# A small transfer ahead of the first load of a row-normalizing kernel

## The chip, the cores and the metric

The kernel runs on one core of one Trainium2 chip. The metric is the device time of one execution in microseconds (us). Before the change it is 81.85 us (median of 3 runs, 81.74 to 81.93). Every time of a whole kernel quoted below is a median of executions in the fast state; a span, a landing or a packet is read from a single profile. A ratio is the mean time of one kernel's fast runs over that of the other's of the same rounds, so it is not quite the ratio of the medians that stand beside it. The span of a profile is shorter than the device time (79.9 us against 81.77 us in the profiled run of before). A profile is a single execution; as the experiments will show, spans of such single executions differ by 0.1 to 0.2 us without any difference in the medians.

## The reference

```python
def setup_inputs():
    batch, dim = 1024, 4096
    return {"x": np.random.randn(batch, dim).astype(np.float32), "axis": -1, "eps": np.float32(1e-12)}

def reference(x, axis, eps):
    norm = np.sqrt(np.sum(x ** 2, axis=axis, keepdims=True) + eps)
    return (x / norm).astype(np.float32)
```

Each of 1024 rows of 4096 numbers is divided by its own length: 16.8 MB are read and 16.8 MB written.

## The kernel before

The rows are cut into two groups of 512, four rows on each of 128 partitions. Each group is one load of 8.4 MB and one store of 8.4 MB, both issued by SyncE. All of x fits into on-chip memory, so no buffer is ever waited for. In the profiles DVE is VectorE, ACT is ScalarE and POOL is GpSimd; a q behind an engine's name (SPq, ACTq, PEq) marks its instruction queue, from which transfers are issued. `to_front` moves both load instructions into the program's entry block, ahead of the barrier at which the engines meet, so that SyncE issues them as its first two instructions.

```python
eps_t = scratch_pool.tile([P, 1], F32)
nc.vector.memset(eps_t, eps)
sq_act = scratch_pool.tile([P, D], F32)
sq_dve = scratch_pool.tile([P, D], F32)
scratch = {"act": sq_act, "dve": sq_dve}

groups = []
for i in range(n_tiles):                       # n_tiles = 2
    g = RowGroups(nc, io, stats, scratch, D, R, eps_t)
    load = nc.sync.dma_start(out=g.flat(), in_=x_t[i])
    to_front(nc, load.ins)
    groups.append(g)

for i, g in enumerate(groups):
    # ... squares with row sums on ACT and DVE, square root, reciprocal, scaling ...
    store = nc.sync.dma_start(out=out_t[i], in_=g.flat())
```

## Time and profile before

| quantity, from the profile of before | value |
|---|---|
| span | 79.9 us |
| DVE busy, ACT busy | 26.7 us (33%), 29.7 us (37%) |
| data moved, mean rate | 33.55 MB, 420 GB/s |
| SyncE's issue of the first load | 0 to 0.38 us |
| first packets begin | from 1.0 us |
| landing of the first load (first squares start) | 21.81 us |
| landing of the second load | 41.14 us |
| first store issued, second store issued | 38.7 us, 56.5 us |

A transfer is carried by 16 DMA engines. Each takes 8 packets of 64 KB of it, then a completion write of 4 bytes. An issue is the SyncE instruction that starts a transfer; its record in the profile doesn't contain the movement of the data. The prediction below shows the lines that bear on this and how to read them. The head is its word for the part of the first load's time in which the DMA engines are not yet full. What it calls a ring is one DMA engine's part of an issuing engine's queue.

### The profile page before, as it was taken

The page shows a single profiled execution, that of the slowest core. Times are in us where ns is not written, and L with a number is a line of the kernel's source. Part 1 is how long each engine was busy: PE and PEld are TensorE (multiplying, and loading weights), DVE is VectorE, ACT ScalarE, POOL GpSimd, SP SyncE. Part 2 cuts the span into 40 slices and gives each one's busy share as a digit, 9 for nine tenths or more (in the row PEclk, how much of TensorE's full clock was granted, in tenths as well). Part 3 has the DMA queues.
Part 4 walks back from the last instruction along what each step waited for, and adds up shares of the span by engine and source line. Part 5 has one row for each costly group of instructions (what it writes and reads, how often), then busy time and mean ns, then how long its engine had stood idle before and what let it go on. Part 6 is the DMA issues. An engine that isn't in the chain of part 4 may idle for free.

```text
span 79.9 us, 93 instructions
## 1 busy us (share of the span) xinstructions
DVE 26.7 (33%) x21; ACT 29.7 (37%) x23; POOL 0.2 (0%) x4
## 2 busy tenths in 40 slices
DVE  0000000000099599960049995999200000000000
ACT  3200000000099999989349999950000000000000
POOL 1000000000000000000000000000000000000000
DMA  9099996599996699993899991999974999965990
GB/s 492 33 525 525 525 525 295 230 525 525 525 525 262 262 525 525 525 525 164 361 525 525 525 459 66 525 525 525 525 328 197 525 525 525 525 295 230 525 525 0
DMA packets 576, 33.55 MB, mean 420 GB/s; under 512 B 64, under 2 KB 64, under 8 KB 64
## 3 DMA queue, kind: packets, MB, share of 16 engines
q1 hardware_dynamic: 576, 33.55, 97.6%
HBM read 16.78 MB, written 16.78 MB: 420 GB/s over the span
## 4 chain that ended last, share of the span: by engine, by line
DMA 51%; ACT 10%; DVE 9%; SPq 0%; issue 0%
DMA xt<-in_x_dram 51%; ACT sq_act L33 9%; DVE xt L64 9%; ACT rstd L53 1%; SPq L219 0%; DVE rstd L59 0%
## 5 line engine op out<-in xcount | busy, mean ns | idle before, releaser
L33 ACT ACTIVATE sq_act<-xt 128x4096 f32<-128x4096 f32 x6 | 21.7, 3609 | 21.7 <-DMA xt<-in_x_dram 21.7
L42 DVE SCALAR_TENSOR_TENSOR sq_dve<-xt 128x4096 f32<-128x4096 f32 x2 | 8.8, 4424 | 25.7 <-DMA xt<-in_x_dram 25.7
L64 DVE TENSOR_SCALAR xt<-xt,rstd 128x4096 f32<-128x4096 f32 x7 | 16.5, 2353 | 0.2
L72 ACT ACTIVATE xt<-xt,rstd 128x3584 f32<-128x3584 f32 x1 | 3.3, 3282 | 0.2 <-DVE rstd L59 0.2
L53 ACT ACTIVATE rstd<-ssq,eps_t 128x1 f32<-128x1 f32 x8 | 2.1, 289 | 0.1
L59 DVE RECIPROCAL rstd<-rstd 128x1 f32<-128x1 f32 x8 | 1.3, 159 | 2.4 <-ACT rstd L53 2.4
L33 ACT ACT_TABLE_LOAD x1 | 1.3, 1283 | 1.3 <-PEq L257 1.3
L53 ACT ACT_TABLE_LOAD x1 | 1.3, 1283 | 0.0
L33 ACT ACTIVATION_READ_ACCUMULATOR sq_act<-xt 128x1 f32 x6 | 1.1, 186 | 0.0
L211 DVE MEMSET eps_t<- 128x1 f32 x1 | 0.1, 59 | 1.3 <-PEq L257 1.3
L78 DVE TENSOR_SCALAR xt<-xt,rstd 128x512 f32<-128x512 f32 x1 | 0.5, 486 | 0.0
L42 DVE DVE_READ_ACCUMULATOR sq_dve<-xt 128x1 f32 x2 | 0.2, 82 | 0.0
L257 POOL MEMSET const-bfloat16-1.0<- 128x1 bf16 x1 | 0.1, 103 | 0.0
L257 POOL MEMSET const-uint8-127<- 128x1 uint8 x1 | 0.1, 102 | 0.0
L257 POOL MEMSET const-float32-0.0<- 128x1 f32 x1 | 0.1, 100 | 0.2 <-issue 0.2
L257 POOL MEMSET const-float32-1.0<- 128x1 f32 x1 | 0.1, 99 | 0.0
## 6 DMA issues: line engine op xcount, KB each, us to landing
xt<-in_x_dram SPq DMA_DIRECT2D x2, 31.2
out_dram<-xt SPq DMA_DIRECT2D x2, 22.5
```

What stands on the lines that cost most here:

```text
L33: self.nc.scalar.activation(out=sq_a, in_=self.x[:, r], func=ACT_F.Square, accum_out=self.ssq[:, r : r + 1],)
L42: self.nc.vector.scalar_tensor_tensor(out=sq_v, in0=self.x[:, r], scalar=1.0, in1=self.x[:, r], op0=ALU.mult, op1=ALU.mult, accum_out=self ...
L53: self.nc.scalar.activation(out=self.rstd[:, r : r + n], in_=self.ssq[:, r : r + n], func=ACT_F.Sqrt, bias=self.eps_t,)
L59: self.nc.vector.reciprocal(out=self.rstd[:, r : r + n], in_=self.rstd[:, r : r + n])
L64: self.nc.vector.tensor_scalar_mul(out=self.x[:, r], in0=self.x[:, r], scalar1=self.rstd[:, r : r + 1])
L72: self.nc.scalar.activation(out=self.x[:, r, :cut], in_=self.x[:, r, :cut], func=ACT_F.Copy, scale=rstd,)
L78: self.nc.vector.tensor_scalar_mul(out=self.x[:, r, cut:], in0=self.x[:, r, cut:], scalar1=rstd)
L211: nc.vector.memset(eps_t, eps)
L257: nc = _bacc.Bacc("TRN2", target_bir_lowering=False, num_devices=1)
```

## The change

A tile of 16 partitions by 128 numbers (512 bytes each, 8 KB together) is loaded from the first rows of x by the same queue, ahead of both loads. Nothing reads the tile. The intent can only be to let the small transfer pay whatever a queue's first use costs, so that the large load finds the queue awake.

```diff
     scratch = {"act": sq_act, "dve": sq_dve}
+
+
+    first = scratch_pool.tile([16, D // 32], F32)
+    to_front(nc, nc.sync.dma_start(out=first, in_=x[:16, : D // 32]).ins)
 
     groups = []
```

## The prediction

> **What bounds the kernel now.** I read four things in this order: the page's table of DMA issues and its chain of work, then the DMA share by long stretches, then the same view in short stretches at the head of the span and at the three borders between transfers, then what the DMA issues and their landings look like.
>
> The chain of work that ended last, and two rows of the page:
>
> ```profile
> ## 4 chain that ended last, share of the span: by engine, by line
> DMA 51%; ACT 10%; DVE 9%; SPq 0%; issue 0%
> ...
> xt<-in_x_dram SPq DMA_DIRECT2D x2, 31.2
> out_dram<-xt SPq DMA_DIRECT2D x2, 22.5
> ```
>
> The chain runs load, load, squares and scalings of the second group, second store. It is misleading: it says that arithmetic (ACT 10%, DVE 9%) holds the end, because the last store's issue waits for the last scaling. But that store was issued at 56.5 us and took 23.3 us to land, for 8.4 MB. It stood behind the first store. So I looked at what the DMA engines do meanwhile. The columns of the next view are: stretch, its length, busy time of DVE, ACT and POOL with their number of instructions, granted clock, DMA share (1.00 is all 16 engines busy), GB/s.
>
> ```profile
> 0.00:4.00 4.00, 0.06 (x1) 1.28 (x1) 0.20 (x4) 1.00 0.74 262
> 4.00:20.90 16.90, 0.00 (x0) 0.00 (x0) 0.00 (x0) 1.00 1.00 434
> 20.90:40.20 19.30, 12.45 (x10) 16.55 (x12) 0.00 (x0) 1.00 1.00 435
> 40.20:59.60 19.40, 14.23 (x10) 11.87 (x10) 0.00 (x0) 1.00 1.00 432
> 59.60:78.90 19.30, 0.00 (x0) 0.00 (x0) 0.00 (x0) 1.00 1.00 435
> ```
>
> From 4 us to 78.9 us all 16 DMA engines are full, through both loads and both stores. The bound is the one DMA queue, at 435 GB/s. The page counts 576 packets for 33.55 MB, 64 of them under 512 B (the completion writes, 16 for each of four transfers); so 512 data packets of 65,536 B, 8 for each engine and transfer. Arithmetic is hidden. Only the head is not full, so the head is what the change can touch. In short stretches (this view books a packet, with its bytes and its whole duration, where it begins, so a share above 1 is normal):
>
> ```profile
> 0.00:1.00 1.00, 0.00 (x0) 0.00 (x0) 0.20 (x4) 1.00 0.00 0
> 1.00:1.30 0.30, 0.00 (x0) 0.04 (x1) 0.00 (x0) 1.00 7.24 2403
> 1.30:1.60 0.30, 0.06 (x1) 0.30 (x1) 0.00 (x0) 1.00 1.13 437
> 1.60:2.10 0.50, 0.00 (x0) 0.50 (x1) 0.00 (x0) 1.00 0.91 393
> ...
> 4.00:4.60 0.60, 0.00 (x0) 0.00 (x0) 0.00 (x0) 1.00 4.03 1748
> ```
>
> Bytes give the number of packets that begin: 2403 GB/s x 0.30 us / 65,536 B = 11, then 2, then 3: the 16 first packets. Share times length times 16 engines over that number gives their mean duration: 7.24 x 0.30 x 16 / 11 = 3.16 us for the 11 early ones, 2.71 us for the two, 2.43 us for the last three. In the stretch from 4.0 to 4.6 us 16 packets begin, of 4.03 x 0.60 x 16 / 16 = 2.42 us. So 2.42 us is the steady time, and the early first packets take 0.74 us longer. An engine that begins at 1.1 us and takes 3.16 us ends at 4.3 us; one that begins at 1.9 us and takes 2.43 us ends at 4.3 us too. Read as steady packets, data flows from about 1.9 us on every engine, however early its first packet began.
>
> **The head in numbers.** The first squares start on the first load's landing, at 21.81 us. Eight steady packets are 8 x 2.42 = 19.3 us. The head is the rest, 2.5 us: the issue, 0.38 us, then 0.6 us until packets begin (1.0 us), 0.9 us until data flows, and 0.4 us to 0.6 us for the spread of the engines and the completion. The issue's row:
>
> ```profile
> L219 SPq DMA_DIRECT2D xt<-in_x_dram x2: 383/404/426, 0.0 to 0.4; - x2
> ```
>
> **What the Trainium skill says.** "DMA: Bandwidth & Descriptors", Queues, rings and completion order: what one sequencer issues goes to one ring on each DMA engine, and descriptors are consumed in ring order. The trace agrees as far as it goes: at 20.9 to 21.5 us, with the first load's last packets ending, 16 packets of the second begin (4.04 x 0.60 x 16 / 16 = 2.42 us each), nothing between. So the small transfer really is ahead of the load on every ring it touches. The same page, on why a DMA increments its semaphore by 16: the slowest dimension decides how many engines take part, and 16 rows give all 16. So each engine would get one row of 512 B and a completion write. No run here shows this yet. "Perfetto Trace Analysis", DMA Instruction — HWDGE: the issue's record covers the wait for the descriptor generator and the making of descriptors, not the data. The trace agrees: the record ends at 0.38 us, the first packet begins after 1.0 us. The DMA page's Specifications give some 0.6 us to the first byte on this path; here it is 1.0 - 0.38 = 0.6 us.
>
> **The change, part by part.** Nothing is removed. The order of instructions shows the one addition, on SyncE, ahead of the two loads; no compute engine's order changes, and both loads and stores keep shape and place. Nobody on the way to the stores waits for the small tile.
>
> Added, the issue: the four issues here take 0.34 to 0.43 us although all carry the same 128 rows, so I have no row for 16. I take the same cost, some 0.38 us plus the 0.05 us that lies between the two loads' issues (0.00 to 0.86 us for 383 + 426 ns): 0.43 us. The loads' issues move back by that, on the path.
>
> Added, the data: 512 B on each engine, at 65,536 B in 2.42 us, is 0.02 us. The completion write costs little at a border: transfers follow each other at 19.33 us (landings 21.81 and 41.14) against 19.34 us for eight packets, so nothing of size hides there. Together under 0.05 us.
>
> Moved: the start barrier behind the issues comes 0.4 us later, so the table load on ACT starts at 1.7 us instead of 1.26 us. It is needed at 21.8 us; it costs nothing.
>
> Possible gain: the 0.9 us between the first packet's beginning and the flow. If this is a first-use cost of the rings or of memory, the small packets start at 1.0 us, pay it until 1.9 us, and the load, whose packets can begin at 1.4 us, flows from 1.9 us. Then the late issue is hidden: 0 to +0.1 us. If it is the ordinary latency of any read at an idle ring, the load pays it again from 1.4 us: +0.43 us. If the small transfer costs less to issue and takes the whole cost away, the load flows from 1.4 us: -0.5 us.
>
> Since the queue is full from there on, whatever the head gains or loses moves all four transfers by as much. The arithmetic moves with the first landing: the first store is issued at 38.7 us, with load packets running to 40.8 us, so there is about 1 us of reserve after its own issue and start latency, and it keeps that when both move together.
>
> **The rivals.** (a) *Plain addition*, +0.4 us, 82.3 us. For it: three of the first packets, begun last, took only 2.43 us, so there is no fixed price for a ring's first packet; early packets seem merely to wait for something that comes at the same distance from the issue, which would move with the issue. (b) *First-use cost absorbed*, about 81.9 us: the ends of all first packets lie within half a microsecond however they began, which suits one common event started by the first packet of all. (c) *Warm-up pays*, 81.3 to 81.5 us: this is what the change hopes for. Against it: SyncE issues one after the other, so the load can't begin before 1.4 us. (d) *The completion write of the small transfer holds the load's packets* until its data is confirmed, +0.5 to 1 us, 82.4 to 82.9 us: against it stand the borders, where packets of the next transfer follow without a gap. (e) *A bound elsewhere*: none is in sight, since compute is 33% and 37% of the span.
>
> **Range and chances.** I weigh (a) 0.45, (b) 0.3, (c) 0.15, (d) 0.1. The mean is +0.45 x 0.4 + 0 - 0.15 x 0.45 + 0.1 x 0.8, about +0.2 us: 82.0 us. Eight in ten: 81.4 to 82.6 us, with 0.1 us for the spread of the runs. Two per cent are 1.64 us. To win that, the head of 2.5 us would have to shrink to 0.9 us, less than issue plus first byte; to lose it, the small transfer would have to cost four issues. Within 2%: 0.97; faster 0.01; slower 0.02.
>
> **What would show each step.** In the changed profile: three issues on SyncE ahead of everything, each of about 0.4 us (a short first one proves my issue cost wrong); 16 more packets of 512 B and 16 completion writes, beginning at 1.0 us; the load's first packets beginning at 1.4 us or later. Their mean duration decides between the rivals: 3.0 us again for (a), near 2.4 us for (b) and (c); steady packets from about 2.3 us for (a), 1.9 us for (b), 1.4 us for (c). The first squares start at 22.2, 21.9 or 21.4 us, the second load lands 19.3 us later in each, and the end moves by the same. If the second landing or the stores move by something else, then the claim that the queue is one full pipe is wrong.

## The result, and the profile after

The changed kernel takes 82.36 us (82.21 to 82.69, 6 runs) against 81.86 us (81.74 to 81.93, 6 runs) in the same rounds. The ratio is 1.0066 with a 95% interval of 1.0047 to 1.0085. So it is slower by about half a microsecond: clear of the noise, but well within 2%. The span of the profiled run grew from 79.94 us to 80.38 us, by 0.44 us. (That run, at 82.21 us, was the fastest of the six.)

The start of the changed kernel's timeline (start, duration, both in us, then what ran):

```profile
0.00 0.39 SPq L218 DMA_DIRECT2D first<-in_x_dram  x1
...
0.44 0.89 SPq L223 DMA_DIRECT2D xt<-in_x_dram  x2
1.74 1.28 ACT L33 ACT_TABLE_LOAD   x1 [1.74 <-PEq L261]
...
22.24 3.62 ACT L33 ACTIVATE sq_act<-xt 128x4096 f32<-128x4096 f32 x1 [19.22 <-DMA xt<-in_x_dram]
```

The small issue takes 0.39 us of SyncE's time, as much as a load of 8.4 MB, and the first load's issue starts at 0.44 us instead of 0. The first load then lands at 22.24 us instead of 21.81 us: 0.43 us later. From its own issue to its landing it takes 21.80 us, as before. The table load on ACT, which waits for the start barrier, came 0.47 us later and cost nothing.

The DMA engines at the head of the changed kernel (columns as in the prediction: stretch, length, DVE, ACT, POOL, clock, DMA share, GB/s):

```profile
1.00:1.40 0.40, 0.00 (x0) 0.00 (x0) 0.00 (x0) 1.00 0.09 21
1.40:1.90 0.50, 0.06 (x1) 0.16 (x1) 0.00 (x0) 1.00 6.28 2097
1.90:4.00 2.10, 0.00 (x0) 1.12 (x1) 0.00 (x0) 1.00 0.00 0
4.00:4.50 0.50, 0.00 (x0) 0.00 (x0) 0.00 (x0) 1.00 0.00 0
4.50:5.00 0.50, 0.00 (x0) 0.00 (x0) 0.00 (x0) 1.00 4.84 2097
```

The small packets begin at 1.0 us, where the load's packets began before. They are tiny: a share of 0.09 over 0.40 us is 0.036 us for each engine, completion write included. The load's 16 first packets begin between 1.4 and 1.9 us (2097 GB/s x 0.50 us / 65,536 B = 16), and their mean duration is 6.28 x 0.50 x 16 / 16 = 3.14 us. So the waiting that made the first packets long before is there in full; before, the mean of all 16 was (11 x 3.16 + 2 x 2.71 + 3 x 2.43) / 16 = 2.97 us. The second packets begin between 4.5 and 5.0 us, against 4.0 to 4.6 us before.

From there on nothing differs. The long stretches, each set some 0.45 us later than those of before:

```profile
0.00:4.50 4.50, 0.06 (x1) 1.28 (x1) 0.20 (x4) 1.00 0.70 235
4.50:21.40 16.90, 0.00 (x0) 0.00 (x0) 0.00 (x0) 1.00 1.00 434
...
60.05:79.40 19.35, 0.00 (x0) 0.00 (x0) 0.00 (x0) 1.00 1.00 434
```

The page's count of packets went from 576 to 608: 16 of 512 B and 16 completion writes, so the small transfer did use all 16 engines.

```profile
DMA packets 608, 33.56 MB, mean 418 GB/s; under 512 B 80, under 2 KB 96, under 8 KB 96
```

### The profile page after: what moved, and what is told of

Read it like the earlier page. It is cut to its first block, busy times and chain, and to the rows that moved or that the text cites. A ratio compares the mean times of both kernels' runs of the same rounds, so it can differ in the third digit from the quotient of the medians.

```text
span 80.4 us, 95 instructions
## 1 busy us (share of the span) xinstructions
DVE 26.7 (33%) x21; ACT 29.7 (37%) x23; POOL 0.2 (0%) x4
## 4 chain that ended last, share of the span: by engine, by line
DMA 51%; ACT 10%; DVE 9%; SPq 1%; issue 0%
DMA xt<-in_x_dram 51%; ACT sq_act L33 9%; DVE xt L64 9%; ACT rstd L53 1%; SPq L223 1%; SPq L218 0%; DVE rstd L59 0%
```

## The experiments

My theory after this result: the change costs the time that SyncE takes to issue one more transfer ahead of the first load, and next to nothing else. It takes nothing away from the load's start. The rivals: the small packets or their completion writes hold what is behind them (D); or a gain from the warm-up exists, and the late issue ate it (W). Ten kernels were run. Those of one batch ran on one chip and share the runs of before: 81.81 us (9 runs) for the first three below and the one with the second load behind the barrier, 81.78 us (7 runs) for the pair behind the barrier, the changed addresses and the first load in halves, 81.89 us (7 runs) for the last two.

### The small transfer between the two loads

```diff
         groups.append(g)
+        if i == 0:
+            first = scratch_pool.tile([16, D // 32], F32)
+            to_front(nc, nc.sync.dma_start(out=first, in_=x[:16, : D // 32]).ins)
```

> The same small transfer, issued between the two loads instead of ahead of both. Theory (the cost is SyncE's issue time ahead of the first load): the first load is issued at 0 again and lands at 21.8 us as before; the second load's issue is hidden; the time is that of before, +0.02 to +0.1 us for 512 B and a completion write on each engine between the loads' packets. Rival (the small transfer's packets or its completion write hold the packets behind them): +0.4 to +0.5 us, now seen as a gap between the two loads' packets at 21 us.

Measured: 81.93 us, ratio 1.0017 (1.0004 to 1.0030). The added 0.12 us of the medians is a quarter of the change's cost. The transfer is the same and its packets run on the same engines; only the order of two issues differs. The first squares of this profile start at 21.93 us, 0.12 us later than in before's, though nothing extra is ahead of that load: this is the spread between single profiles. Between the last packet of the first load and the first of the second the trace shows some 0.03 us on each engine, where the small packet and the second completion write lie. So the data of a small transfer costs about 0.03 us here, and D falls as the explanation of 0.5 us for a queue that is already busy. For the start of an idle queue, the runs behind the barrier, below, decide.

### Two small transfers ahead

```diff
     to_front(nc, nc.sync.dma_start(out=first, in_=x[:16, : D // 32]).ins)
+    more = scratch_pool.tile([16, D // 32], F32)
+    to_front(nc, nc.sync.dma_start(out=more, in_=x[16:32, : D // 32]).ins)
```

> Two small transfers ahead of the first load. Theory: two issues of 0.39 us and their gaps, so 0.89 to 0.93 us more than before and the first load's packets from 1.9 us on, about 82.8 us. Rival (a once-only cost or a partly absorbed start): the second one costs clearly less or more than the first, which cost 0.44 us of the span.

Measured: 82.78 us against 81.81 us, ratio 1.0112 (1.0097 to 1.0128). The medians differ by 0.97 us, twice the change's 0.50 us.

```profile
0.00 0.39 SPq L218 DMA_DIRECT2D first<-in_x_dram  x1
...
0.44 0.41 SPq L220 DMA_DIRECT2D more<-in_x_dram  x1
0.90 0.90 SPq L225 DMA_DIRECT2D xt<-in_x_dram  x2
```

The first load is issued at 0.90 us. The cost grows with the issues ahead of it; the second small transfer costs what the first one did, so nothing of the first one's cost was made good by a once-only gain.

### The small transfer on ScalarE's queue

```diff
-    to_front(nc, nc.sync.dma_start(out=first, in_=x[:16, : D // 32]).ins)
+    to_front(nc, nc.scalar.dma_start(out=first, in_=x[:16, : D // 32]).ins)
```

(In this run `to_front` was changed too: it places an instruction in the entry block of the engine that issues it, where before it always took SyncE's place.)

> The same small transfer, issued at the front of ScalarE's queue, so that SyncE issues the first load at once. Theory: within 0.1 us of before, as SyncE's issue of 0.39 us is off the path. Rival 1 (data or completion on the engines costs): +0.4 us stays, as the small packets still run on all 16 engines around 1 us. Rival 2 (a warm-up gain exists, and was eaten by the issue): 0.2 to 0.7 us faster than before, first packets of 2.4 us instead of 3.0 us.

Measured: 81.88 us against 81.81 us, ratio 1.0003 (0.9991 to 1.0016), the same. With SyncE's time free, the cost is gone.

One premise of this run failed. The issue on ScalarE:

```profile
L218 ACTq DMA_DIRECT2D first<-in_x_dram x1: 376/376/376, 0.1 to 0.1; - x1
...
DMA to landing us min/median/max: 7.3/7.3/7.3
```

It was issued at 0.1 us and landed only 7.3 us later. In the trace each engine ran the 512-byte packet after its first 64 KB packet of the load, from 4.03 us on, and the completion write one 64 KB packet later. So the small transfer was not ahead of the load's first packets, and this run says nothing on W. It does show that the packets and completion writes of a small transfer, in the midst of the load, cost nothing that the time shows.

### Both loads behind the start barrier, without and with the small transfer

For W the small transfer must have finished before the load starts, in time that is waited anyway. The barrier offers that time. The control moves both loads behind it; the second run has, besides, the small transfer ahead of it.

```diff
         load = nc.sync.dma_start(out=g.flat(), in_=x_t[i])
-        to_front(nc, load.ins)
```

> Control for the next run: before's kernel with both loads issued after the start barrier, no small transfer. The first load's issue comes some 0.5 to 0.7 us later against the other engines' first instructions; 82.2 to 82.6 us. From the first load's issue to its first packets 1.0 us, first packets 3.0 us on average, to the landing 21.8 us, as in before.

> The small transfer issued at 0, both loads after the start barrier (about 0.8 us), so that it runs and nearly lands before the first load's packets begin (about 1.8 us), and its issue lies in time that the barrier takes anyway. Theory (no first-use cost exists that a small transfer can take away): from the first load's issue, packets begin 1.0 us and the landing comes 21.8 us later, first packets 3.0 us; the time is that of the control, within 0.2 us. Rival (a first-use cost exists, and in the change the load followed too closely): first packets near 2.4 us, landing 0.4 to 0.9 us nearer to the issue, and 0.3 to 0.9 us faster than the control.

Measured: 82.48 us for the control (ratio to before 1.0075, 1.0052 to 1.0097) and 82.59 us with the small transfer (1.0092, 1.0063 to 1.0122). The small transfer brings no gain. The control's timeline, then that with the small transfer:

```profile
0.73 0.85 SPq L219 DMA_DIRECT2D xt<-in_x_dram  x2
...
22.52 3.62 ACT L33 ACTIVATE sq_act<-xt 128x4096 f32<-128x4096 f32 x1 [20.50 <-DMA xt<-in_x_dram]
```

```profile
0.80 0.82 SPq L223 DMA_DIRECT2D xt<-in_x_dram  x2
...
22.53 3.62 ACT L33 ACTIVATE sq_act<-xt 128x4096 f32<-128x4096 f32 x1 [20.45 <-DMA xt<-in_x_dram]
```

From the first load's issue to its landing it is 21.79 us in the control and 21.73 us with the small transfer, where W asked for 0.4 to 0.9 us less. The first packets of the load in the two runs, the control's first:

```profile
1.70:2.60 0.90, 0.00 (x0) 0.31 (x1) 0.00 (x0) 1.00 3.43 1165
```

```profile
1.00:1.30 0.30, 0.00 (x0) 0.30 (x1) 0.00 (x0) 1.00 0.11 28
1.70:2.60 0.90, 0.00 (x0) 0.38 (x1) 0.00 (x0) 1.00 3.48 1165
```

Each 1165 GB/s line holds 16 packets, so their means are 3.43 x 0.90 = 3.09 us and 3.48 x 0.90 = 3.13 us. In the second run all small packets had begun by 1.3 us on the same rings and the tile had landed by 1.5 us, before any load packet began. The load's packets were as long all the same. W falls: with the ring used by a small transfer some 0.3 us earlier, the start costs what it did. D falls for the idle queue as well: here the small packets and their completion writes did run ahead of the load, and of the 0.11 us between the two medians some 0.07 us is the load's later issue (0.80 us against 0.73 us). The control also gives the price of a late issue once more: 0.73 us later, 0.70 us slower.

### What makes the first packets long

That left the question what the extra 0.55 us in the first packets (2.97 us against 2.42 us) are. Three runs without any small transfer asked. The first moved only the second load behind the barrier, so that its issue doesn't fall into the first packets' time:

```diff
-        to_front(nc, load.ins)
+        if i == 0:
+            to_front(nc, load.ins)
```

> Before's kernel with the second load issued after the start barrier (about 1 to 1.6 us) rather than at 0.43 us; no small transfer. It asks what makes the first packets take 3 us instead of 2.4 us. If it is the second load's issue, which runs just when the first packets begin: first packets near 2.4 us and 0.3 to 0.6 us faster. If not: first packets near 3 us again and within 0.1 us of before.

Measured: 81.83 us against 81.81 us, ratio 1.0004 (0.9991 to 1.0017). The mean of the first packets is 3.01 us in the trace. The second load's issue is not the cause. The span of this profile is 0.2 us longer than before's at the same median time: this is the size of what a single profile leaves open.

The second changed the addresses, so that neighbouring partitions read 64 KB apart rather than 128 KB:

```diff
-    x_t = x.rearrange("(p t r) d -> t p (r d)", t=n_tiles, r=R)
-    out_t = out_flat.rearrange("(p t r) d -> t p (r d)", t=n_tiles, r=R)
+    x_t = x.rearrange("(t p r) d -> t p (r d)", t=n_tiles, r=R)
+    out_t = out_flat.rearrange("(t p r) d -> t p (r d)", t=n_tiles, r=R)
```

> Before's kernel with each load covering one contiguous half of the rows, so neighbouring partitions read 64 KB apart instead of 128 KB. It asks whether the long first packets (3.0 us) come from the engines all starting at once on addresses with that spacing. If so: first packets' mean moves clearly from 3.0 us, and the time with it, by 0.1 to 0.5 us. If not: first packets 3.0 us, time within 0.1 us of before.

Measured: 82.10 us against 81.78 us, ratio 1.0035 (1.0004 to 1.0066), with a first-packet mean of 3.11 us. The spacing does not make them short. That the kernel became slower by some 0.3 us was not followed up.

The third cut the first load into two transfers, with packets of 32 KB:

```diff
+        if i == 0:
+            half = R * D // 2
+            for k in range(2):
+                cols = slice(k * half, (k + 1) * half)
+                load = nc.sync.dma_start(out=g.flat()[:, cols], in_=x_t[i][:, cols])
+                to_front(nc, load.ins)
+        else:                                   # the load as it was
```

> The first load issued as two transfers of half the columns each, packets of 32 KB on its two halves. It asks whether the first packets' extra time is a fixed one or grows with the packet. Fixed (a start latency of about 0.6 us): first packets of 1.2 + 0.6 = 1.8 us, the flow from 1.9 us as in before, time within 0.1 us of before. Proportional (slow rate during the first packet, 3.0 / 2.4): first packets of 1.5 us, the flow 0.3 us earlier.

```profile
0.99:2.20 1.21, 0.06 (x1) 0.47 (x1) 0.00 (x0) 1.00 1.46 433
2.70:3.30 0.60, 0.00 (x0) 0.31 (x1) 0.00 (x0) 1.00 2.02 874
```

Both lines hold 16 packets of 32 KB. The first ones take 1.46 x 1.21 = 1.77 us, the next ones 2.02 x 0.60 = 1.21 us. The difference of the means is 0.55 us again, so the extra time doesn't grow with the packet. On this point the run was clear. Its time was a surprise: 83.12 us against 81.78 us, ratio 1.0152 (1.0125 to 1.0179), though the first load landed as in before.

### An early store

In that run the order of the arithmetic changed with the landing of the halves, and the first store was issued at 31.8 us instead of 38.7 us. The last packet of the second load on each engine took 3.6 us instead of 2.42 us. Two runs were to tell the store from the halves. The first keeps the halves and repeats a square twice in the first group, to put the store off:

```diff
-        g.square_act(2)
+        for _ in range(3 if i == 0 else 1):
+            g.square_act(2)
```

> The run with the first load in halves was 1.2 to 1.3 us slower than before, though its load packets flowed as in before: the last load packets of each engine took 3.6 us instead of 2.42 us. Its first store had been issued at 31.8 us instead of 38.7 us. Here the halves stay, and two repeated squares of one row (their result is the same) put the store off to about 39 us. If the early store is what stretched those packets: 2.42 us again and within 0.2 us of before. If the halves are: 3.6 us and 83.1 us again.

Measured: 82.99 us against 81.89 us, ratio 1.0135 (1.0119 to 1.0150). This run missed its aim: its store was issued at 36.9 us, not at 39 us, which was still before the last load packets began (37.7 us). They took 3.6 us again, so it tells nothing apart.

The second has whole loads as in before; in the first group two of the four rows stay unscaled, so its result is wrong, and its first store is issued at 32.1 us:

```diff
-        g.square_act(1)
-        g.norm(1)
+        if i > 0:
+            g.square_act(1)
+            g.norm(1)
         g.norm(R - 1)
-        g.scale(1)
+        if i > 0:
+            g.scale(1)
         g.scale(R - 1)
-        ...                                     # row 2 squared and scaled, by both engines if i is 0
+        if i > 0:
+            ...                                 # row 2 squared and scaled
```

> Before's kernel with whole loads, but the first group leaves two of its four rows unscaled (a wrong result on purpose), so that its store is issued at about 30 us. If an early store stretches the last load packets: 3.6 us there and about 83 us, with nothing else changed in the transfers. If the halves did it: 2.42 us and within 0.2 us of before.

Measured: 82.91 us against 81.89 us, ratio 1.0121 (1.0104 to 1.0138). The last packets of the second load, in before and in this run:

```profile
37.85:38.35 0.50, 0.00 (x0) 0.50 (x1) 0.00 (x0) 1.00 4.85 2097
```

```profile
37.80:38.30 0.50, 0.00 (x0) 0.00 (x0) 0.00 (x0) 1.00 7.02 2097
```

They take 4.85 x 0.50 = 2.43 us in before and 7.02 x 0.50 = 3.51 us here. The early store does it without the halves; that the halves add something of their own is not excluded (their loss was 1.3 us in the first run, 1.1 us in the second). Before's store is issued at 38.7 us, after those packets have begun, and costs nothing. Why a store that already waits in the queue stretches the last load packet by 1.1 us stays open. For the change it plays no part: there the store and the load's last packets moved by the same 0.4 us, and those packets took 2.43 us as before. No version tried beats the kernel before.

## Why the prediction was right or wrong, by its steps

- **The bound** was right. The queue is full from the head to the end, and the head's delay reached the end undiminished: 0.43 us at the first landing, 0.44 us at the end of the span. The control behind the barrier shows the same: 0.73 us later at the issue, 0.71 us at the first landing, 0.70 us in the time.
- **The issue**, estimated at 0.43 us with its gap from the loads' issues, measured 0.44 us (0.39 us and a gap of 0.05 us). With some 0.04 us of data it accounts for 0.48 us of the 0.50 us between the medians; the interval of the ratio allows 0.38 to 0.70 us. A transfer of 16 rows costs SyncE as much as one of 128 rows of 64 KB.
- **The data**, under 0.05 us, was right: 0.036 us of packets on each engine, and some 0.03 us at the border between the loads.
- **The barrier and the table load** moved by 0.47 us where 0.4 us was stated, and cost nothing, as predicted.
- **The reserve of the first store** was read as harmless if both move together, and they did. What I had not seen is that this reserve must not grow too far: with whole loads, a first store issued at 32.1 us cost 1.0 us.
- **The rivals**: rival (a), the plain addition of 0.4 us to 82.3 us, is what happened, at 82.36 us. It had a weight of 0.45. Rivals (b), absorption, and (c), warm-up, are refuted by the pair behind the barrier, and (d), the completion write, by the same pair and by the small transfer between the loads. The marks I had set for (a) came in: landing at 22.24 us (22.2 foretold), first packets at 3.14 us (3.0 again), the load's packets from 1.4 us on.
- **The reason given for (a)** held. It read the three first packets of 2.43 us, begun last, as a sign that the early ones wait for something at a constant distance from the issue. They were no accident of that profile. The first packets that begin after 1.8 us, in the run on ScalarE's queue and in that with the second load late:

```profile
1.80:2.20 0.40, 0.00 (x0) 0.40 (x1) 0.00 (x0) 1.00 0.77 328
1.80:2.20 0.40, 0.00 (x0) 0.27 (x1) 0.00 (x0) 1.00 0.78 328
```

Each line holds two packets, of 0.77 x 0.40 x 16 / 2 = 2.46 us and 2.50 us. In the changed kernel all 16 begin between 1.4 and 1.9 us, so none is so late after its load's issue, and all wait. Taking the last 2.42 us of each first packet as its data (an estimate), the data begin 2.42 us before the second packets do: 1.6 to 2.2 us after the load's issue in before, 1.6 to 2.1 us in the changed kernel, and about the same in the control. That distance is what stayed, and it moved with the issue.

- **The number** 82.0 us was 0.36 us too low, inside the range of 81.4 to 82.6 us. The mis-sized term is the mixture: 0.45 of the weight went to absorption and gain, which turned out to be nothing. The range held (a), (b) and parts of (c) and (d), so that the time fell into it says little; what singles out (a) are the marks and the experiments. The statement of within 2% was right.

What stays open is what the first packets of a large transfer wait for, 0.55 us on the mean in before. It is not something that a small transfer on the same rings takes away (the pair behind the barrier), not the second load's issue, not the address spacing tried, and not proportional to the packet. Whether an earlier large transfer would take it away was not tried.

## What to carry to other kernels

In this kernel, whose DMA queue is full from the head to the end, what the issuing engine did ahead of the first load was added to the time about one for one (issues of 0.44 and 0.90 us cost 0.50 and 0.97 us); a useless transfer of 8 KB cost as much issue time as one of 8.4 MB. A warm-up has to be tried in two places: where it delays the real work, and where it costs nothing; only the second tells whether it warms anything. If a small transfer must be had, issue it behind the first load or from another engine's queue, where it was free to within 0.12 us here.

## What the Trainium skill lacked or had wrong

- "DMA: Bandwidth & Descriptors" gives the cost of a DMA issued from GpSimd as a fixed part and a part by size, but no issue time on SyncE for this chip outside a comparison in its section on the later chip. Here the issue took 0.39 us for 16 rows of 512 B and 0.38 us for 128 rows of 64 KB, and it was nearly the whole cost of the change.
- The same page, Specifications, gives about 0.6 us to the first byte on this path. The first packets' records agree if it is counted from the end of the issue, which the page doesn't say (they begin 0.6 us after it). But a large load on an idle queue then lost another 0.55 us on the mean of its first packets, the same for packets of 64 KB and 32 KB; no page that I read has it.
- The same page, Queues, rings and completion order, says that an engine switches between queues only at packet boundaries. The run on ScalarE's queue agrees, if the page's packets are those of the trace, and shows what it means beside a large load: 8 KB landed 7.3 us after their issue, since each small packet and each completion write stood behind a 64 KB packet of 2.42 us or longer.
- No page that I read has the cost of a store that is queued early behind a load: the last load packet of each engine took 3.51 us instead of 2.43 us, and the kernel lost 1.0 us.
